# One pinned split instead of two in the expert stage of a hybrid mLSTM / RWKV-7 / MoE layer

## The chip, the cores and the metric

The kernel runs on one core of a Trainium2 chip. The metric is the device time of one execution in microseconds (us), with the median over several runs. Beside the times there is one profiled execution, whose trace gives each instruction's start and duration on TensorE (matrix products), VectorE, ScalarE, GpSimd and SyncE (which issues most transfers).

## The reference, cut to what matters

The layer is a backbone layer over 2048 latent tokens of 1024 channels with 256 context tokens: a modulated layer norm, one input projection, an mLSTM group and an RWKV-7 group, an output projection, and then a mixture of experts. The change touches only the last of these. There are 32 experts; each token goes to two of them, with weights `w`:

```python
    def expert_block(args):
        idx, w, e = args
        xb = tok_pad[idx]
        hb = jax.nn.silu(xb @ ex_gate[e]) * (xb @ ex_up[e])
        return (hb @ ex_down[e]) * w[:, None]
...
    y = lax.map(expert_block, (tok_buf.reshape(n_blk, MOE_BLOCK), w_buf.reshape(n_blk, MOE_BLOCK), blk_exp))
    out = jnp.zeros((n + 1, d), y.dtype).at[tok_buf].add(y.reshape(buf, d))
```

`ex_gate[e]` and `ex_up[e]` are 1024 x 512, `ex_down[e]` is 512 x 1024, all in float32. The result of each expert's block is added to its tokens' rows, and a layer norm follows.

## The kernel before, in words

**Precision.** A float32 product is made from three products of rounded halves. Each operand A is split into a high part H (a copy on ScalarE that rounds) and a low part L = A - H (a subtraction on VectorE); the product is H·H + H·L + L·H, three matmuls on TensorE, added up in one PSUM tile.

**Weights.** An expert has six raw tiles of 1 MB (gate 2, up 2, down 2), which SyncE loads from HBM into a pool of seven (`ER`), each when an earlier tile of the pool has been used up. Each raw tile gives two pieces of 128 x 1024 (`split`, lines 1525 to 1533: the copy is line 1531, the subtraction line 1532), so an expert has twelve: 0 to 3 for gate, 4 to 7 for up, 8 to 11 for down. H and L parts lie in pools of thirteen buffers each (`EH`), so piece i of an expert takes the buffer of piece i-1 of the expert before.

**An expert's round.** `moe` loops over the 32 experts in Python, fully unrolled. For a block of 128 gathered tokens, `gate_up` makes the gate product (8 steps over the channels), the Silu on ScalarE into `act`, and the up product in two column halves. When the first up half is complete, `mult(0)` on VectorE multiplies it into `act` (line 1622); two transposes of that half on TensorE, the copy `aH` on ScalarE and the subtraction `aL` on VectorE (lines 1540, 1548, 1553) make the operand for the first two steps of the down product. `mult(1)` does the same for the second half. `tail` makes the down product in four steps, each with one down piece, with the transposes of the next expert's tokens (`fill`) after the first step; the result is scaled and added to the tokens' rows in HBM by GpSimd (`add`).

**More than 128 tokens.** Where an expert has more tokens, further blocks run with the same pieces inside a runtime branch (`tc.If(nx > 0)`, line 1737) that stands between `gate_up` and the tail of the last block. Every engine passes this branch. In the data used, twelve of the 32 experts take it, and some of these have more than one further block.

**Order.** Every engine works through its own queue in order. A planner (the framework's scheduler) puts the instructions of the straight code in that order by its own estimates of when each is ready; among instructions that are ready, what is traced earlier stands to go first. The program forces it in places: `behind()` and `tc.issue_after(ins)` put what is traced inside them behind `ins` on the engine of `ins` alone, and on no other engine.

**Where the pieces are split.** At the end of a round, pieces 0 to 7 of the next expert are traced (`AHEAD` is 8): 0 and 1 in no forced place, 2 to 7 behind the last split of `act`. At the start of the next round the pieces up to number 9 follow in no forced place (line 1706). The rest, pieces 10 and 11, come from `more(2, m)` in `gate_up` (line 1609): their VectorE subtractions are pinned behind `m`, which is `mult(0)`; their ScalarE copies are not.

Of the kernel before, what the change touches and what calls it, by code (L numbers as in the profile page):

```python
# [53 lines left out]
class Kern:  # L54
# [1442 lines left out]
    def moe(self):  # L1497
        tc, nc, I, s = self.tc, self.nc, self.I, self.scratch
        with ExitStack() as es:
# [25 lines left out]
            def split(R, i):  # L1525

                w = R[i // 2]
                hk = w.shape[1] // 2
                w = w[:, hk * (i % 2):hk * (i % 2) + hk, :]
                H, L = hp.tile(list(w.shape), FR, name="eH"), hp.tile(list(w.shape), FR, name="eL")  # L1530
                self.cp = nc.scalar.copy(H, w)  # L1531
                nc.vector.tensor_tensor(L, w, H, op=OP.subtract)  # L1532
                return H, L

            def split_T(A, src, g, step, own=False, after=None, later=False):

                ps = (pu if own else pt).tile([128, 4, 128], F, name="epx" if own else "ept")
                for k in range(step):
                    kk = step * g + k
                    self.pe = nc.tensor.transpose(ps[:, k, :], src[:, 128 * kk:128 * kk + 128], self.ident)  # L1540
                    if after:
                        tc.add_manual_dep(self.pe.ins, after.ins.name,
                                          mybir.DependencyInfo(mybir.DependencyClass.NoSync, mybir.DependencyReason.DATA),
                                          reason="the expert's own products go first")
                ks = slice(step * g, step * g + step)

                def split(order=None):
                    self.lastc = nc.scalar.copy(A[0][:, ks], ps[:, :step])  # L1548
                    if order:
                        tc.add_manual_dep(self.lastc.ins, order.ins.name,  # L1550
                                          mybir.DependencyInfo(mybir.DependencyClass.NoSync, mybir.DependencyReason.DATA),
                                          reason="the block's own work goes first")
                    self.last = nc.vector.tensor_tensor(A[1][:, ks], ps[:, :step], A[0][:, ks], op=OP.subtract)  # L1553

                if later:
                    return split
                split()

            def parts(pool, n, nm):
                return tuple(pool.tile([128, n, 128], FR, name=nm + x, bufs=1) for x in "HL")  # L1560

            def mm(o, A, W, k, kw, c, first, last):
                H, L = W
                for i, (a, b) in enumerate(((A[0], H), (A[0], L), (A[1], H))):
                    self.pe = nc.tensor.matmul(o, a[:, k, :], b[:, kw, c], start=first and i == 0, stop=last and i == 2)  # L1565

            def behind():

                return tc.issue_after(self.pe.ins) if self.pe else ExitStack()
# [6 lines left out]
            def load_ids(dst, src):  # L1576
                ld = nc.gpsimd.dma_start(dst, src)
                for sc in self.scat:
                    behind_dma(ld, sc, "entries of the token table")

            def gather(x, ids):
                return nc.gpsimd.indirect_dma_start(out=x, out_offset=None, in_=self.H2,
                                                    in_offset=bass.IndirectOffsetOnAxis(ap=ids, axis=0))

            def gate_up(X, W, R=None):

                def more(n, behind):
                    if R:  # L1590
                        with tc.issue_after(behind.ins):
                            for _ in range(n):
                                W.append(split(R, len(W)))

                g = pu.tile([128, DE], F, name="epg")
                for k in range(8):
                    mm(g, X, W[k // 2], k, k % 2, slice(0, DE), k == 0, k == 7)
                nc.scalar.activation(act, g, AF.Silu)

                def up(k, h):  # L1600
                    mm(us[h][:, 0:256], X, W[4 + k // 2], k, k % 2, slice(256 * h, 256 * h + 256), k == 0, k == 7)

                for k in range(3):
                    for h in range(2):
                        up(k, h)
                for k in range(3, 8):
                    up(k, 0)
                m = mult(0)
                more(2, m)
                with behind():  # L1610
                    for k in range(3, 6):
                        up(k, 1)
                with behind():
                    split_T(Aa, act, 0, 2)
                with behind():
                    for k in range(6, 8):
                        up(k, 1)
                mult(1)

            def mult(h):  # L1620
                c = act[:, 256 * h:256 * h + 256]
                return nc.vector.tensor_tensor(c, c, us[h][:, 0:256], op=OP.mult)
# [36 lines left out]
            Rs = {0: load_raw(0)}  # L1659
            W = [split(Rs[0], i) for i in range(AHEAD)]  # L1660
# [36 lines left out]
            for e in range(NE):  # L1697
                nx, x1 = coming

                with behind():  # L1700
                    tc.mark_branch_hint_location("e%d" % e, hint=nx, engines=[PE])
                cur = ids[:, 0, e]
                act = bp.tile([128, DE], F, name="act")
                Aa = parts(bp, 4, "a")
                us = [pu.tile([128, 512], F, name="epu%d" % h) for h in range(2)]
                W += [split(Rs[e], i) for i in range(len(W), 10)]
                if left:
                    add(*left)
                with behind() if e == 0 else ExitStack():
                    gate_up(X, W, Rs[e])  # L1710
                last = self.pe

                def extra(i):


                    if not isinstance(i, int) or i > 1:
                        new = ap.tile([128, 2], I32, name="more")
                        load_ids(new, self.TB[bass.ds((i + (16 * e + 1)) * 128, 128), :])
                        gather(x1, new[:, 0:1])
                    else:  # L1720
                        new = ids[:, 1 + i, e]
                    old = ap.tile([128, 2], I32, name="old")
                    nc.vector.tensor_copy(old, cur)
                    nc.vector.tensor_copy(cur, new)
                    self.pe = None
                    Z = parts(xp, 8, "z")

                    def mid():
                        with tc.If(nx > 1):
                            gather(x1, ids[:, 2, e, 0:1])  # L1730

                    add(tail(W, lambda g: split_T(Z, x1, g, 4, later=g == 0), mid if isinstance(i, int) and i == 0 else None), old)
                    gate_up(Z, W)

                if e + 1 < NE:
                    coming = begin(e + 1, order)
                with tc.If(nx > 0, label="e%d" % e):  # L1737
                    tc.mark_branch_hint_location("f%d" % e, hint=nx - 1, engines=[PE])
                    extra(0)
                    with tc.If(nx > 1, label="f%d" % e):  # L1740
                        extra(1)
                        with tc.If(nx > 2):
                            with tc.For_i(2, nx, 1) as i:
                                extra(i)

                def fill(g):
                    nonlocal x
                    if e + 1 < NE:
                        late = split_T(X, x, g, 4, True, last, g == 0)
                    else:  # L1750
                        late = None
                    if g == 1 and e + 2 < NE:
                        x = fetch(ids[:, 0, e + 2, 0:1])
                    return late

                self.pe = None
                X = parts(xp, 8, "x")
                left = tail(W, fill), cur
                order = self.last
                if e + 2 < NE:  # L1760
                    Rs[e + 2] = load_raw(e + 2)
                if e + 1 < NE:
                    W = [split(Rs[e + 1], i) for i in range(2)]
                    with tc.issue_after(self.evac[0]), tc.issue_after(self.evac[1]):
                        W += [split(Rs[e + 1], i) for i in range(2, AHEAD)]
# [84 lines left out]
```

## Time and profile before

| | |
|---|---|
| median of 3 runs | 3421.06 us (3416.99 to 3427.79) |
| profiled execution: its time / its span | 3418.58 us / 3417.0 us |
| TensorE (matmul) busy | 2866.9 us, 84% |
| VectorE busy | 2339.6 us, 68% |
| ScalarE busy | 1364.0 us, 40% |
| GpSimd busy | 879.0 us, 26% |
| expert stage in the trace | about 2305 to 3351 us |
| splits in it, line 1531 / line 1532 | 384 x 1052 ns / 384 x 1221 ns |

Busy shares are averages over stages with different limits. The expert stage is read by itself, in windows of one expert's round. In a timeline row the numbers are the start and the length in us, and the bracket gives the idle time of the engine before the instruction and what ended it. "xN" in a row means N instructions in a row, merged. Where a suffix q stands behind an engine's name, it is that engine's sequencer, which takes branches and sends semaphore events.

### The profile page before, as it was taken

To read this page: it belongs to the slowest core of one execution; us is meant where nothing else is said; L and a number is where in the kernel's file an instruction comes from. 1 tells how busy PE (TensorE), PEld (TensorE's weight loads), DVE (VectorE), ACT (ScalarE), POOL (GpSimd) and SP (SyncE) were. 2 spreads that over 40 slices of the span, in tenths; PEclk is the share of its full clock that TensorE was granted. 3 is DMA by queue.
4 is the path that set the end of the run, shared out by engine and by line. 5 is a ranking of instruction groups with operands and counts; after the bars stand their busy time and mean duration, and the time that the engine had idled before them with its cause. 6 is when DMAs were issued, how large, how long until landed. Compare 5 with 4: busy or idle time off the path is not lost. (4 is left out here: it accounts for less than half of the span.)

```text
span 3417.0 us, 61401 instructions
## 1 busy us (share of the span) xinstructions
PE 2866.9 (84%) x24042; PEld 2405.9 (70%) x24042; DVE 2339.6 (68%) x3822; ACT 1364.0 (40%) x2187; POOL 879.0 (26%) x862
## 2 busy tenths in 40 slices
PE   6899999999979964777777588859899989989992
PEld 3677788898757754666666567647778877878781
DVE  4488888766787875667656288875877736476447
ACT  4432322335545322334344233344655525355233
POOL 5400000013455660112112365431222212122210
PEclk9899999999979875778788789979999999999996
DMA  5333332235468534666664554448988848597535
GB/s 187 117 114 108 101 116 82 88 101 189 164 219 242 167 109 115 171 159 170 155 168 128 159 174 137 141 147 286 334 295 284 304 125 276 159 335 234 177 112 209
DMA packets 471689, 602.59 MB, mean 176 GB/s; under 512 B 127222, under 2 KB 312338, under 8 KB 471314
## 3 DMA queue, kind: packets, MB, share of 16 engines
q1 hardware_dynamic: 413617, 441.15, 41.2%
q0 software_dynamic: 36736, 129.33, 13.0%
q10 hardware_dynamic: 20960, 27.20, 2.5%
q8 instruction: 224, 3.67, 0.5%
q14 instruction: 152, 1.24, 0.1%
HBM read 453.24 MB, written 144.33 MB: 175 GB/s over the span
## 5 line engine op out<-in xcount | busy, mean ns | idle before, releaser
L1532 DVE TENSOR_TENSOR eL<-eraw,eH 128x1024 fp32r<-128x1024 f32 x384 | 449.6, 1221 | 28.6 <-ACT eH L1531 24.6
L329 DVE SCALAR_TENSOR_TENSOR cacc<-P,cw,cacc 128x1008 f32<-128x1008 f32 (+3 forms) x320 | 398.7, 1247 | 56.5 <-ACT cacc L304 45.6
L1531 ACT CAST eH<-eraw 128x1024 fp32r<-128x1024 f32 x384 | 370.9, 1052 | 48.3 <-PEq L1737 35.1
L263 PE MATMUL in_ps<-hH,w_H 128*128 128x512 f32 (+1 forms) x664 | 252.3, 382 | 1.7 <-ACT pl_ev L355 1.7
L263 PE MATMUL in_ps<-hL,w_H 128*128 128x512 f32 (+1 forms) x664 | 249.6, 377 | 0.0
L263 PE MATMUL in_ps<-hH,w_L 128*128 128x512 f32 (+1 forms) x664 | 248.0, 374 | 0.0
L1565 PE MATMUL epo<-eH,aH 128*128 128x512 f32 x408 | 172.2, 422 | 64.8 <-DVEq L1737 32.2
L1651 POOL DMA_INDIRECT ACC<-yo,ids x32 | 131.0, 4093 | 250.5 <-DVE yo L1650 226.1
L1565 PE MATMUL epo<-eH,aL 128*128 128x512 f32 x408 | 159.7, 404 | 11.7 <-DVE aL L1553 11.7
L1565 PE MATMUL epo<-eL,aH 128*128 128x512 f32 x408 | 163.2, 400 | 0.0
L931 PE MATMUL rpg<-KR,BK 64*128 64x128 f32 (+1 forms) x1152 | 122.4, 350 | 46.7 <-ACT BT L941 17.5
L237 POOL DMA_DIRECT2D w_raw<-in_w_in x28 | 21.2, 757 | 506.2 <-DVE w_L L251 371.8
L263 PEld LDWEIGHTS in_ps<-hH,w_H 128*128 128x128 f32 x664 | 126.2, 191 | 34.6 <-issue 11.5
L931 PEld LDWEIGHTS rpg<-KR,BK 64*128 64x128 f32 x1152 | 104.9, 248 | 63.2 <-issue 23.8
L973 DVE TENSOR_TENSOR sT<-sM,sY 128x31 f32<-128x31 f32 (+15 forms) x279 | 95.3, 342 | 78.8 <-DMA sM<-BL 70.8
L298 ACT COPY P<-in_ps 128x512 f32<-128x512 f32 (+1 forms) x92 | 51.3, 557 | 235.8 <-PE in_ps L263 235.8
L1565 PE MATMUL epu<-eH,xL 128*128 128x256 f32 x512 | 143.4, 283 | 0.0
L1565 PE MATMUL epu<-eL,xH 128*128 128x256 f32 x512 | 143.2, 283 | 0.0
L263 PEld LDWEIGHTS in_ps<-hL,w_H 128*128 128x128 f32 x664 | 126.2, 190 | 22.7 <-issue 2.1
L1565 PE MATMUL epu<-eH,xH 128*128 128x256 f32 x512 | 142.2, 288 | 0.0
L263 PEld LDWEIGHTS in_ps<-hH,w_L 128*128 128x128 f32 x664 | 126.1, 190 | 22.3 <-issue 0.8
L1565 PEld LDWEIGHTS epo<-eH,aH 128*128 128x128 f32 x408 | 78.9, 193 | 83.1 <-ACT xH L1548 30.7
(471 smaller groups left out, 8151.1 us busy)
## 6 DMA issues: line engine op xcount, KB each, us to landing
eraw<-in_ex_gate SPq DMA_DIRECT2D x64, 1024.0 KB
eraw<-in_ex_up SPq DMA_DIRECT2D x64, 1024.0 KB
eraw<-in_ex_down SPq DMA_DIRECT2D x64, 1024.0 KB
pk<-PK SPq DMA_DIRECT2D x144, 320.0 KB
PK<-pk POOLq DMA_DIRECT2D x36, 768.0 KB, 3.9
ada_w<-in_w_ada SPq DMA_DIRECT2D x32, 512.0 KB
v<-MV SPq DMA_DIRECT2D x50, 264.0 KB
kc<-KTd SPq DMA_DIRECT2D x50, 256.0 KB
```

Source lines behind the costliest of these rows:

```text
L237: self.wld = nc.gpsimd.dma_start(w[:, 4:8, o:o + cn], src[:, 4:8])
L263: nc.tensor.matmul(o, a[:, k, :], b, start=i == 0, stop=i == 3 * KT - 1)
L298: nc.scalar.copy(P[:, t0:t0 + n], ps)
L329: nc.vector.scalar_tensor_tensor(o, img[:, r0 + sy:r1 + sy, c0 + sx:c1 + sx], wt(dy, dx), o, op0=OP.mult, op1=OP.add)
L931: nc.tensor.matmul(pG[e][:, q, b.cols], b.BK[HD[e], c, q, :], b.KR[HD[e], c, q, b.cols], start=True, stop=True, tile_position=(64 * e, 0))
L973: nc.vector.tensor_tensor(tt, M[:, 0:j, j:j + 1].to_broadcast([128, j, w]), Y[:, j:j + 1, j:32].to_broadcast([128, j, w]), op=OP.mult)
L1531: self.cp = nc.scalar.copy(H, w)
L1532: nc.vector.tensor_tensor(L, w, H, op=OP.subtract)
L1565: self.pe = nc.tensor.matmul(o, a[:, k, :], b[:, kw, c], start=first and i == 0, stop=last and i == 2)
L1651: nc.gpsimd.indirect_dma_start(out=self.ACC, out_offset=bass.IndirectOffsetOnAxis(ap=cur[:, 0:1], axis=0), in_=y, in_offset=None, compute_ ...
```

## The change

One number goes from 2 to 1 and one from 10 to 11. In `gate_up`, one piece (11) and not two has its subtraction pinned behind `mult(0)`. At the start of a round, three pieces (8, 9 and 10) and not two are traced in no forced place, ahead of `add` and `gate_up`. Nothing is computed differently, and the number of instructions stays the same.

```diff
@@ gate_up
                 for k in range(3, 8):
                     up(k, 0)
                 m = mult(0)
-                more(2, m)
+                more(1, m)
                 with behind():
                     for k in range(3, 6):
                         up(k, 1)
@@ the loop over the experts
                 us = [pu.tile([128, 512], F, name="epu%d" % h) for h in range(2)]
-                W += [split(Rs[e], i) for i in range(len(W), 10)]
+                W += [split(Rs[e], i) for i in range(len(W), 11)]
                 if left:
                     add(*left)
```

The function that `gate_up` calls for the pinned pieces, unchanged:

```python
def more(n, behind):
    if R:
        with tc.issue_after(behind.ins):
            for _ in range(n):
                W.append(split(R, len(W)))
```

## Rows read from the trace of the kernel before

**Rows 1.** Windows of one round: length, busy per engine, PEclk, DMA share, GB/s.
```profile
2425.70:2446.30 20.60, 18.25 (x110) 15.95 (x110) 17.86 (x21) 13.68 (x17) 5.54 (x3) 1.00 1.04 355
...
2671.50:2692.20 20.70, 18.35 (x111) 16.02 (x110) 17.89 (x22) 13.68 (x17) 7.61 (x4) 1.00 1.04 374
```

**Rows 2.** Waits of TensorE, expert stage: who waited for whom, us, times, longest.
```profile
PE epo L1565 <- DVEq L1737: 32.2, 14, 2.4
PE epo L1565 <- PEq L1737: 14.8, 3, 5.1
...
PE epo L1565 <- DVE aL L1553: 11.7, 12, 1.0
PE epo L1565 <- ACT eH L1531: 7.0, 3, 2.4
```

**Rows 3.** Timeline of the last expert, VectorE, ScalarE and TensorE.
```profile
3342.20 2.35 DVE L1532 TENSOR_TENSOR eL<-eraw,eH 128x1024 fp32r<-128x1024 f32 x2
...
3343.09 0.37 ACT L1548 CAST aH<-ept 128x256 fp32r<-128x256 f32 x1 [3.77 <-PE ept L1540]
...
3344.47 0.42 DVE L1553 TENSOR_TENSOR aL<-ept,aH 128x256 fp32r<-128x256 f32 x1
...
3345.42 0.47 PE L1565 MATMUL epo<-eH,aH 128*128 128x512 f32 x1 [1.66 <-DVEq L1737]
```

**Rows 4.** Timeline of an expert with a further block, TensorE's wait.
```profile
2574.97 0.50 PE L1565 MATMUL epo<-eH,aL 128*128 128x512 f32 x1 [0.97 <-DVE aL L1553]
```

**Rows 5.** Timeline of a round without a further block, from mult(0) on.
```profile
2466.97 0.42 DVE L1622 TENSOR_TENSOR act<-act,epu 128x256 f32<-128x256 f32 x1 [1.05 <-PE epu L1565]
...
2467.31 3.49 DVE L1532 TENSOR_TENSOR eL<-eraw,eH 128x1024 fp32r<-128x1024 f32 x3
...
2467.78 0.38 PE L1540 MATMUL ept<-ident,act 128*128 128x128 f32 x2
...
2468.20 0.37 ACT L1548 CAST aH<-ept 128x256 fp32r<-128x256 f32 x1 [2.82 <-PE ept L1540]
...
2470.72 0.42 DVE L1553 TENSOR_TENSOR aL<-ept,aH 128x256 fp32r<-128x256 f32 x1
2471.05 0.41 DVE L1622 TENSOR_TENSOR act<-act,epu 128x256 f32<-128x256 f32 x1
...
2471.66 0.47 PE L1565 MATMUL epo<-eH,aH 128*128 128x512 f32 x1 [2.35 <-DVEq L1737]
...
2475.65 0.40 PE L1565 MATMUL epg<-eH,xL 128*128 128x512 f32 x1
...
2476.09 2.36 DVE L1532 TENSOR_TENSOR eL<-eraw,eH 128x1024 fp32r<-128x1024 f32 x2 [0.16 <-ACT eH L1531]
```

**Rows 6.** Line 1737 (the branch) in that round: duration ns, first and last start.
```profile
L1737 PEldq EVENT_SEMAPHORE  x1: 51/51/51, 2469.4 to 2469.4; - x1
...
L1737 DVEq EVENT_SEMAPHORE  x1: 21/21/21, 2471.5 to 2471.5; - x1
```

**Rows 7.** Timeline of the copies and of VectorE ahead of mult(0); last expert's copies.
```profile
2617.59 10.54 ACT L1531 CAST eH<-eraw 128x1024 fp32r<-128x1024 f32 x11
2628.03 0.59 ACT L1598 ACTIVATE act<-epg 128x512 f32<-128x512 f32 x1
...
2625.69 3.49 DVE L1532 TENSOR_TENSOR eL<-eraw,eH 128x1024 fp32r<-128x1024 f32 x3
2630.22 0.42 DVE L1622 TENSOR_TENSOR act<-act,epu 128x256 f32<-128x256 f32 x1 [1.04 <-PE epu L1565]
...
3329.23 9.60 ACT L1531 CAST eH<-eraw 128x1024 fp32r<-128x1024 f32 x10
```

**Rows 8.** Windows of 2 us after a 2.35 us wait, columns as in rows 1.
```profile
2494.00:2496.00 2.00, 2.00 (x9) 1.67 (x9) 0.08 (x1) 0.33 (x1) 0.09 (x1) 0.50 0.99 308
2496.00:2498.00 2.00, 2.00 (x8) 1.57 (x7) 1.55 (x4) 2.00 (x4) 0.91 (x1) 0.69 1.05 410
```

**Rows 9.** Timeline of SyncE: issue of the next gate's two tiles.
```profile
2612.32 3.50 SPq L1518 DMA_DIRECT2D eraw<-in_ex_gate  x2
```

## The prediction, made before the change was run

> **What bounds the kernel now.** The profiled execution takes 3418.58 us, 1.58 us of it outside its span of 3417.0; the median of the three runs shown is 3421.06, so 2.48 is added at the end. The diff touches the expert stage alone, about 2305 to 3351 us. I read the busy time by window first, to see what an expert's round is made of. A round of an expert without a further block (20 of the 32) takes 20.6 us, of which TensorE is busy 18.25 and VectorE 17.86, at the full 2.4 GHz clock, while the DMA share stands above 1 [rows 1]. So three things are nearly full and none is quite full; what decides is the wait between two of them.
>
> The view of waits says which. TensorE waits 32.2 us in 14 pieces for VectorE's queue at line 1737, the branch around the further block, 7.0 us in three pieces put down to a copy on ScalarE, and 11.7 us in twelve pieces for `aL` [rows 2]. The single waits show what the totals hide: every one of the first two kinds is 2.35 us, in 16 experts, but for the last expert's 1.66 [rows 3]; each of the twelve experts with a further block waits 0.97 or 0.98 [rows 4]; and three experts wait for TensorE's own branch, 14.8 us in all [rows 2], where nothing on VectorE matters.
>
> The timeline of one round shows the 2.35 [rows 5]. `mult(0)` starts on VectorE at 2466.97. Behind it stand three subtractions of a split, 3.49 us together, then `aL`, then `mult(1)`, and only when that is over does VectorE pass the branch: its semaphore event is at 2471.5, TensorE's own at 2469.4 [rows 6]. TensorE starts the down products at 2471.66. ScalarE's `aH` had ended at 2468.57, so `aL`, and `mult(1)` behind it, stood about 2.1 us behind splits that the block doesn't need yet. The three late "ScalarE" waits start TensorE 0.61 us after `mult(1)` as the others do, so I count them as the same wait.
>
> **Which three splits these are.** ScalarE makes eleven copies without a gap and then the Silu [rows 7]; in the last expert, which has no successor, it makes ten, and only two subtractions stand behind `mult(0)` [rows 3, 7]. So the eleventh copy, and the third subtraction, is piece 0 of the next expert, and the other two are pieces 10 and 11, which `more(2, m)` pins there. Pieces 8 and 9, free, were put ahead of `mult(0)`.
>
> **The change, part by part.** *The pin.* `issue_after` holds only VectorE's half of a split, so ScalarE's copies were free before and need not move. One subtraction loses its pin. I expect the planner to treat piece 10 as it treated piece 9: it is traced ahead of `gate_up`, its copy is done before the Silu on which `mult(0)` depends, and its buffer (thirteen per half) is that of piece 9 of the expert before, last read in that expert's tail.
>
> *What leaves the path.* Three subtractions take 3.49 us, two take 2.35 [rows 3, 5], so the burst shortens by 1.14.
>
> *What it costs ahead of `mult(0)`.* VectorE is idle there for 1.04 us, waiting for the up products [rows 7]. That idle time is the cover: 1.14 goes into it, and `mult(0)` starts 0.10 later. The transposes that read it start 0.39 us after its end [rows 5], so TensorE does not feel the 0.10; the burst does. Were the cover gone, `mult(0)` would be late by 1.14 and the gain would be nil, since the burst is shorter by as much. Queued behind piece 10 on VectorE are only `mult(0)` and the burst.
>
> *Rounds without a further block.* 1.14 - 0.10 = 1.04 us off each 2.35; sixteen of them give 16.6. The last expert keeps one subtraction of two, but `aL` can't start before `aH` ends (3343.46; it started 1.0 later, behind two subtractions) [rows 3]: 0.95. The last expert is also the test of the step, with the planner's own order: with two subtractions its TensorE waits 1.66 and not 2.35, the 1.14 less but for some 0.45 in which it transposes nothing for a successor.
>
> *Rounds with a further block.* TensorE stands 0.97 for `aL` [rows 4]; `aL` comes 1.04 earlier, so the wait goes: 12 x 0.97 = 11.6. What follows on VectorE there (`mult(1)`, the `zL` halves) moves up with it.
>
> *The three branch waits.* Nothing: they end later than VectorE does.
>
> Sum: 16.6 + 0.95 + 11.6 = 29.2 us.
>
> *Clock.* After five of the sixteen 2.35 us waits TensorE is granted 1.2 GHz for a time. In the one shown two windows of 2 us have 0.50 and 0.69 of full speed, so 1.0 + 0.6 = 1.6 us are lost [rows 8]; five make 8. After the waits of 0.97, of 1.66 and the other ones under 1.8 us it stays at 2.4 GHz throughout. The new waits are 1.3 us, between these, nearer to those without a fall. Bounds 0 and 8; I take 5.
>
> *Transfers.* SyncE's loads are issued when VectorE frees a raw tile, so they come in the same order, each 1 us closer to the next. The round that moves 355 GB/s in 20.6 us (7.3 MB) must then move it in 19.6, 373 GB/s. One round already runs at 374 [rows 1]. What covers a shortfall is the lead of the loads: the tightest, the next gate's first tile, is issued at 2612.32 [rows 9] and copied as the eleventh of the row that begins at 2617.59 and lasts 10.54 [rows 7], so at about 2627: 14.7 us. It and the pair ahead of it, three tiles of 1.05 MB, take about 9 us at 355 GB/s from the earlier issue, so it lands near 2618 and some 9 us are spare. If the DMA can't go faster at all, each round falls 1 us behind; the longest run of rounds without a further block is seven, and a further block lets the loads catch up. Bounds: nothing, and all of the 16.6; I take 2, because the spare time is larger than seven rounds ask for.
>
> The Trainium skill speaks against the change here: "DMA: Bandwidth & Descriptors" (the warning on its three ceilings) has the HBM side, about 358 GB/s per core, bind such loads. By that a round of 7.3 MB needs 20.4 us, and the rounds would give only 0.2 us each once the lead is eaten. The round at 374 does not agree with it as a hard limit.
>
> So 29.2 + 5 - 2 = 32.2: 3418.58 - 32.2 = 3386.4 for the profiled execution, and 2.48 more, **3389 us**, for a median.
>
> **The rivals.** *The planner leaves the order as it is* (10%). If its estimate has `mult(0)` ready before VectorE is through with piece 9, and it takes what is ready by another measure than trace order, piece 10 stays behind `mult(0)` with or without a pin: the same three subtractions, 3421. For it: the next expert's piece 0 was as free as piece 9 and stands behind `mult(0)`. Against it: that piece is traced later than `mult(0)`, piece 10 earlier.
>
> *The loads become the bound* (10%). If the spare 9 us are not there, the rounds stay at 20.6 us, ScalarE waits for the gate's tile in front of the Silu, and only the further blocks and the last expert gain: 12.5 us, 3408.5, right at the edge of what can be told. For it: the DMA share of 1.04 in these rounds [rows 1]. Against it: the gapless row of copies [rows 7], and 374 GB/s.
>
> *Slower, by the gate's products* (8%). TensorE fills the tail with gate products of the next expert; at 2475.65 they run on while VectorE begins pieces 2 and 3 at 2476.09 [rows 5]. Pieces 0 and 1 give ten more products of about 0.23 us, until 2477.9; piece 2 is ready at 2477.3. If the changed plan drew piece 2's products straight to 2475.65, TensorE would wait 1.65 us in every expert: 32 x 1.65 = 53, less the 29 gained, 3421 + 24 = 3445. It decides from 0.9 us per expert on. Against it: the pin that is lost lies 9 us away from these products, and their order needs no change.
>
> **How the numbers follow.** The forecast has 72%, the three rivals 10, 10 and 8. A median of this kernel can be told from no change by about 0.3%, 10.3 us. The forecast lies beyond that, and I give half of the second rival to faster and half to same: faster 0.77, same 0.15, slower 0.08. The likeliest case's own range is 3382 (all 8 of the clock, no loss to the loads) to 3396 (nothing from the clock, 4 lost to the loads). The range takes in the rivals up to no change and the spread of its runs, 3424, and goes to 3378 for a gain that I sized too small; it leaves out the slower rival and a little below.
>
> **What would show it.** Right: two subtractions in one row behind `mult(0)` (2.35 us) and four instead of three ahead of it; TensorE's waits at line 1737 near 1.3 us sixteen times; no wait for `aL` in the twelve; rounds of 19.6 us; fewer windows below full clock; idle before `mult(0)` near zero. Wrong: still three subtractions behind `mult(0)`; waits of ScalarE's copies for the gate's transfer, with gaps in its row of eleven; a new wait of gate products for `eL`; a rise of the idle time before the transposes of `act`, which would say that the 1.04 of cover was less than I took it for.

## The result, and the profile after

The changed kernel takes 3385.86 us (median of 4 runs, 3376.78 to 3389.73) against 3422.27 for the kernel before (4 runs, 3416.99 to 3427.79): a ratio of 0.9894, interval 0.9869 to 0.9919, or 36.4 us less. 3389 was forecast. The profiled execution took 3376.78 us with a span of 3375.1; 9 us of its distance to the one before lie ahead of the expert stage, where nothing was changed, and are the spread of single executions. So I compare the stage by itself. From the first down product of the first expert to that of the last it took 3345.42 - 2322.48 = 1022.9 us before and 3303.34 - 2313.39 = 990.0 after, 32.9 less. The 3.5 us that the medians differ by beyond this are not accounted for; executions of the changed kernel alone lie up to 13 us apart.

The timeline of a round without a further block, from the last splits ahead of `mult(0)` on (it answers to [rows 5, 7]; SyncE, GpSimd, weight loads and the up products are left out):

```profile
2447.70 4.62 DVE L1532 TENSOR_TENSOR eL<-eraw,eH 128x1024 fp32r<-128x1024 f32 x4
2452.26 0.42 DVE L1622 TENSOR_TENSOR act<-act,epu 128x256 f32<-128x256 f32 x1
2452.60 2.35 DVE L1532 TENSOR_TENSOR eL<-eraw,eH 128x1024 fp32r<-128x1024 f32 x2
2453.07 0.38 PE L1540 MATMUL ept<-ident,act 128*128 128x128 f32 x2
2453.48 0.37 ACT L1548 CAST aH<-ept 128x256 fp32r<-128x256 f32 x1 [2.85 <-PE ept L1540]
...
2454.87 0.41 DVE L1553 TENSOR_TENSOR aL<-ept,aH 128x256 fp32r<-128x256 f32 x1
2455.20 0.41 DVE L1622 TENSOR_TENSOR act<-act,epu 128x256 f32<-128x256 f32 x1
...
2455.81 0.47 PE L1565 MATMUL epo<-eH,aH 128*128 128x512 f32 x1 [1.21 <-ACT eH L1531]
```

Four subtractions in a row stand ahead of `mult(0)` and two, 2.35 us, behind it. `mult(0)` follows them with no idle time. TensorE starts the down products 0.61 us after the start of `mult(1)`, as before [rows 5], and has waited 1.21 us instead of 2.35. The view names ScalarE's `eH` as the releaser. That copy, of the next expert's piece 1, ran from 2454.73 to 2455.77, so by this round alone it could be. A kernel further below settles it: with piece 1 moved elsewhere, fifteen such waits are 1.21 to 1.27 us long still, and the view puts them down to VectorE at line 1737.

Three windows of a round (against [rows 1]; busy time of TensorE, weight loads, VectorE, ScalarE, GpSimd, then clock, DMA share, GB/s). The first starts at an expert whose wait was ended by TensorE's own branch:

```profile
2435.31:2455.81 20.50, 18.56 (x108) 15.82 (x109) 17.81 (x22) 14.59 (x19) 6.71 (x2) 1.00 1.04 366
2455.81:2475.38 19.57, 18.32 (x109) 15.98 (x109) 17.82 (x22) 13.72 (x18) 6.70 (x2) 1.00 1.04 366
2475.38:2494.91 19.53, 18.32 (x109) 15.97 (x109) 17.75 (x22) 13.65 (x18) 8.73 (x3) 1.00 1.04 373
```

A regular round takes 19.53 to 19.57 us, 1.1 less than before; the first of the three, with a wait of 0.73 for `xL` in it, takes 20.50. And the view of TensorE's waits in the stage (against [rows 2]):

```profile
PE epo L1565 <- PEq L1737: 20.9, 7, 5.0
...
PE epo L1565 <- ACT eH L1531: 14.7, 12, 1.2
...
PE epx L1540 <- DVE xL L1553: 7.7, 16, 0.7
...
PE epo L1565 <- DVEq L1737: 0.7, 1, 0.7
```

The wait for `aL` is gone. Of the sixteen waits of 2.35 us twelve are now 1.21 to 1.25. The other four stand in the first row, which had three entries before and has seven: experts 5, 12, 19 and 26 now wait 1.48 to 1.75 us for TensorE's own branch, and each of them waits 0.73 more for `xL` a little later. The last row is the last expert, 0.69 instead of 1.66 [rows 3].

ScalarE's row of copies has no gap in this round, so no load came late. In the whole stage one copy waits for a load, the eleventh of the row that ends the longest run of rounds without a further block (last line):

```profile
2439.60 10.54 ACT L1531 CAST eH<-eraw 128x1024 fp32r<-128x1024 f32 x11
2450.03 0.60 ACT L1598 ACTIVATE act<-epg 128x512 f32<-128x512 f32 x1
...
2508.61 1.05 ACT L1531 CAST eH<-eraw 128x1024 fp32r<-128x1024 f32 x1 [0.73 <-DMA eraw<-in_ex_gate]
```

And the clock does not fall after the new waits. This is one of the four longest, 1.73 us up to 2435.31, and the four microseconds behind it, where [rows 8] had 0.50 and 0.69:

```profile
2433.60:2435.30 1.70, 0.00 (x0) 0.02 (x1) 0.99 (x3) 0.16 (x1) 0.00 (x0) 1.00 1.03 408
2435.30:2437.30 2.00, 1.99 (x8) 1.32 (x8) 1.08 (x1) 1.37 (x2) 0.00 (x0) 1.00 1.06 308
2437.30:2439.30 2.00, 1.27 (x9) 1.10 (x9) 0.74 (x2) 0.45 (x1) 0.21 (x1) 1.00 1.06 272
```

### The profile page after: what moved, and what is told of

Same layout as the page of the kernel before. It is cut to its first block, busy times and chain, and to the rows that moved or that the text cites. A ratio compares the mean times of both kernels' runs of the same rounds, so it can differ in the third digit from the quotient of the medians.

```text
span 3375.1 us, 61432 instructions
## 1 busy us (share of the span) xinstructions
PE 2854.0 (85%) x24042; PEld 2395.2 (71%) x24042; DVE 2337.1 (69%) x3822; ACT 1364.7 (40%) x2187; POOL 926.2 (27%) x862
## 3 DMA queue, kind: packets, MB, share of 16 engines
q14 instruction: 153, 1.25, 0.1%
## 5 line engine op out<-in xcount | busy, mean ns | idle before, releaser
L1651 POOL DMA_INDIRECT ACC<-yo,ids x32 | 175.2, 5476 | 240.7 <-DVE yo L1650 240.7
L1582 POOL DMA_INDIRECT xg<-H,ids x48 | 59.6, 1242 | 246.4 <-PE ept L1540 192.4
```

The lines of the kernel that those rows point to most:

```text
L1651: nc.gpsimd.indirect_dma_start(out=self.ACC, out_offset=bass.IndirectOffsetOnAxis(ap=cur[:, 0:1], axis=0), in_=y, in_offset=None, compute_ ...
```

## The experiments

My theory: VectorE's burst behind `mult(0)` sets the wait of each round, and VectorE's idle time ahead of `mult(0)` is what can take a split out of it. Rivals: the length of the burst alone decides, wherever the rest stands; or the gain comes from somewhere else in the stage. Each kernel is set against the kernel before, run beside it on the same chip; each diff is against the changed kernel, unless another is named.

**The change in two halves.** One kernel has it only in the twelve experts with a further block, one only in the other twenty.

```diff
-                more(1, m)
+                more(12 - len(W), m)
...
-                W += [split(Rs[e], i) for i in range(len(W), 11)]
+                W += [split(Rs[e], i) for i in range(len(W), 11 if e in FURTHER else 10)]
```

(`FURTHER` stands for the set 1, 9, 10, 15, 16, 18, 20, 21, 25, 28, 29, 30; the other half has `not in`.)

> The change is made only in the twelve experts that take the further block; the other twenty keep two pinned pieces and ten in no forced place. Theory (each kind of round gains by itself, by the burst behind mult(0)): the twelve waits of 0.97 us for aL go, the sixteen of 2.35 us stay, and with them the falls of the clock: about 12 us faster than before, 3410. Rival (the gain is the planner's new order of gate and down products on TensorE inside the further blocks, which the change brought along): most of the 36 us come here, 3390. Rival (what is gained in one kind of round is lost again at the next wait): no change.

Measured: 3409.92 us (median), ratio 0.9974, interval 0.9962 to 0.9987, 11.9 us less than the 3421.8 before.

> The change is made only in the twenty experts that do not take the further block. Theory: the sixteen waits of 2.35 us shrink to 1.2, except that the four rounds whose branch on TensorE comes late gain little; the clock stays up behind the shorter waits; the twelve waits of 0.97 us stay. About 21 us faster than before (11 from the waits, 1 from the last expert, up to 8 from the clock), 3401, and with the kernel of the other half of the experts it adds up to the whole gain. Rival (order of TensorE's products in the further blocks): nearly nothing, 3420.

Measured: 3397.38 us, ratio 0.9943, interval 0.9921 to 0.9964, 24.4 less. The two gains add up to 36.3, the whole is 36.4. The intervals of the two gains are about 4 and 7 us to either side, so the closeness is luck; but the gain has the two independent sources that the prediction named, and no third one larger than these intervals. TensorE's waits in the second half show the first source used and the second not:

```profile
PE epo L1565 <- ACT eH L1531: 14.6, 12, 1.2
PE epo L1565 <- DVE aL L1553: 11.6, 12, 1.0
```

**Other numbers of splits behind `mult(0)`.** The kernel before has three in a row there and the changed one two, the next expert's piece 0 among them. First, four:

```diff
-                more(1, m)
+                more(3, m)
...
-                W += [split(Rs[e], i) for i in range(len(W), 11)]
+                W += [split(Rs[e], i) for i in range(len(W), 9)]
```

> The opposite dose: three pieces pinned behind mult(0) and nine in no forced place, so four subtractions instead of three stand behind mult(0). Theory: each of the sixteen waits grows from 2.35 to 3.5 us, the twelve for aL from 0.97 to 2.1, the last expert's by 1.1: 33 us slower than before, and up to 10 us more because the clock falls after more of the longer waits: 3455 to 3465. Rival (only the wait at mult(0) counts, and it has slack): no change from before, 3422.

Measured: 3482.47 us, ratio 1.0175, interval 1.0155 to 1.0196. The waits came as expected, and the time did not:

```profile
PE epo L1565 <- DVEq L1737: 62.0, 18, 3.5
PE epo L1565 <- DVE aL L1553: 25.3, 12, 2.1
```

Seventeen waits of 3.48 (the eighteenth is the last expert's 2.79) and twelve of 2.1. What I had set too small was the clock, here in a window of one such wait and the four microseconds behind it:

```profile
2433.26:2436.74 3.48, 0.00 (x1) 0.03 (x1) 3.33 (x6) 1.53 (x2) 0.00 (x0) 1.00 1.02 303
2436.74:2438.74 2.00, 2.00 (x7) 1.61 (x8) 1.77 (x2) 0.00 (x0) 0.00 (x0) 0.74 0.97 305
2438.74:2440.74 2.00, 2.00 (x10) 1.70 (x8) 0.00 (x0) 0.18 (x1) 0.00 (x0) 0.50 1.14 354
```

The grant falls to the lower level, 1.2 GHz, after 14 of the 17 waits of 3.48 and after 11 of the 12 of 2.1. So a split more behind `mult(0)` costs its own 1.14 per round, and the clock on top.

Then none: no piece of the expert's own is pinned, and the next expert's piece 0 stays free.

```diff
-                more(1, m)
+                more(0, m)
...
-                W += [split(Rs[e], i) for i in range(len(W), 11)]
+                W += [split(Rs[e], i) for i in range(len(W), 12)]
```

> No piece pinned and twelve in no forced place; the planner then also draws the next expert's piece 0 ahead of mult(0), so no subtraction at all stands behind it. Theory (what was won is bounded by VectorE's idle time ahead of mult(0), which the change has used up): mult(0) comes 2.3 us later than after the change, the burst ends only 1.0 earlier, so a round takes 20.9 us and the experts with a further block stand 1.9 us before the transposes of act; 40 us slower than after the change, 3425. Rival (the burst alone counts): another 1.1 us off each round, 25 to 30 us faster than after the change, 3358.

Measured: 3448.01 us, ratio 1.0079, interval 1.006 to 1.0099: slower than before, where 3425 was expected. The planner put six splits ahead of `mult(0)`, the next expert's piece 0 among them, and none behind (the profiled execution, of 3471.76 us, is the longest of its five):

```profile
2484.00 6.89 DVE L1532 TENSOR_TENSOR eL<-eraw,eH 128x1024 fp32r<-128x1024 f32 x6
2490.80 0.41 DVE L1622 TENSOR_TENSOR act<-act,epu 128x256 f32<-128x256 f32 x1
2492.15 0.42 DVE L1553 TENSOR_TENSOR aL<-ept,aH 128x256 fp32r<-128x256 f32 x1 [0.94 <-ACT aH L1548]
```

TensorE's wait has moved from the branch to the transposes of `act`, which wait for `mult(0)`. A wait of 0.7 us for `xL` has come in, 27 times, which I had not counted. It is a part of the 23 us by which I was off, 14.9 in all where the change has 7.7 already; the rest I did not take apart:

```profile
PE ept L1540 <- DVE act L1622: 54.2, 31, 1.8
...
PE epx L1540 <- DVE xL L1553: 14.9, 27, 0.7
...
PE epo L1565 <- DVEq L1737: 4.6, 13, 0.7
```

The wait at line 1737 has all but gone, and the kernel is slower than before: the length of the burst is not what decides.

And one: the next expert's piece 0 alone, pinned.

```diff
-                more(1, m)
+                if R: self.m0 = m
...
-                W += [split(Rs[e], i) for i in range(len(W), 11)]
+                W += [split(Rs[e], i) for i in range(len(W), 12)]
...
-                    W = [split(Rs[e + 1], i) for i in range(2)]
+                    with tc.issue_after(self.m0.ins): W = [split(Rs[e + 1], 0)]
+                    W += [split(Rs[e + 1], i) for i in range(1, 2)]
```

> One step further than the change: all of pieces 8 to 11 are traced in no forced place, and the next expert's piece 0 alone is pinned behind mult(0), so that five subtractions stand ahead of mult(0) and one behind it. Theory 1 (VectorE's idle time ahead of mult(0) was the cover, and the change has used it up: 1.04 us before, none after): the fifth subtraction makes mult(0) late by its whole 1.14 us, so the burst of one gains nothing, and the late transposes of act put a wait of their own into each round; as in the run without any pin, a wait of some 0.7 us for xL is added. Rounds of about 20.3 us, against 19.55 for the change; some 24 us slower than the change, about 3410. Theory 2 (what sets the wait is the length of the burst behind mult(0), wherever the rest stands): TensorE's waits at line 1737 go from 1.2 to about 0.1 us and the kernel takes about 3365.

Measured: 3410.9 us, ratio 0.9969, interval 0.9952 to 0.9986. Theory 1 said 3410, theory 2 3365. With five splits ahead of `mult(0)` and one behind, TensorE waits at three places of a round:

```profile
PE ept L1540 <- DVE act L1622: 18.8, 31, 0.7
PE epx L1540 <- DVE xL L1553: 16.3, 28, 0.7
...
PE epo L1565 <- DVEq L1737: 5.0, 13, 0.7
```

So the order of the doses, by splits in a row behind `mult(0)`: none 3448, one 3411, two (the change) 3386, three (before) 3422, four 3482. By this number alone there is nothing more to gain.

**Moving a split to another place.** In the changed kernel the one idle time of VectorE above 0.2 us in a round is ahead of the second half of `xL`:

```profile
2439.47 0.69 DVE L1553 TENSOR_TENSOR xL<-epx,xH 128x512 fp32r<-128x512 f32 x1 [1.43 <-ACT xH L1548]
```

One kernel has piece 1 of the next expert pinned behind the first half of `xL` and `xH`, on both engines, and nothing else:

```diff
-                                late(self.pe)
+                                late(self.pe); self.x0 = self.last.ins, self.lastc.ins
...
-                    W = [split(Rs[e + 1], i) for i in range(2)]
+                    W = [split(Rs[e + 1], 0)]
+                    with tc.issue_after(self.x0[0]), tc.issue_after(self.x0[1]): W += [split(Rs[e + 1], 1)]
```

> The change as it is, with one split moved: piece 1 of the next expert is pinned, on VectorE and on ScalarE, behind the first half of the transposed tokens (xL, xH), into the 1.4 us in which VectorE stands idle between the two halves of xL. The burst behind mult(0) stays at two. Theory 1 (in the four rounds in which TensorE comes late through its own branch, the second wait of 0.73 us for xL arises because piece 1 of the next expert stands ahead of xL): these four waits go, 0.73 x 4 = 2.9 us, and a regular round gains at most 0.1 us: 3 to 6 us faster than the change, about 3381. Theory 2 (xL is late there for the transposes alone): the four waits stay and the time is that of the change, 3386.

Measured: 3365.57 us, ratio 0.9842, interval 0.9819 to 0.9866: the fastest kernel here, 20 us below the change. That is several times what I expected, and only part of it for the reason given. Its waits in the stage:

```profile
PE epo L1565 <- DVEq L1737: 19.2, 16, 1.3
...
PE epo L1565 <- ACT xH L1548: 7.6, 9, 1.7
...
PE epo L1565 <- DVE xL L1553: 5.9, 3, 2.0
PE epo L1565 <- PEq L1737: 2.1, 1, 2.1
```

The waits of the transposes for `xL` are gone, all 7.7 us of them and not the 2.9 of four experts alone. The three entries for `xL` and the one for the branch are the four late experts, whose waits in front of the down product have grown from 6.6 to 8.0 us, so 6.3 of the 7.7 are gained. What I had not expected is that the three waits of 4.7 to 4.95 us for TensorE's branch, in experts 3, 17 and 24, are 1.24 to 1.27 now, some 10.6 us less, and that the falls of the clock behind them are gone with them (two have come in behind the four late experts). A regular round is 19.48 to 19.50 us, hardly shorter than the change's. VectorE's idle time ahead of the second half of `xL` did not fill, it is 1.41 us still: piece 1 now stands between the first half and that idle time, where it stood ahead of the first half.

The two edits together, one split behind `mult(0)` and piece 1 behind the first `xL`:

> Both of the two edits: one subtraction behind mult(0) instead of two, and piece 1 of the next expert moved into VectorE's idle time between the halves of xL, so that there is again one subtraction fewer ahead of mult(0). Theory 1 (the change's rule goes on as long as mult(0) is not late): mult(0) starts on time, the wait at line 1737 falls from 1.2 to about 0.1 us, rounds take about 18.6 us, and the kernel takes about 3370. Rival (the loads become the bound): a round moves 7.3 MB, which in 18.6 us is 393 GB/s, above the 374 seen so far; then ScalarE's row of eleven copies shows gaps in front of the next gate's tile and the rounds stay at 19.3 us or more: 3382 or above. Second rival (the cover is used up all the same, since the rounds get shorter by as much as VectorE was relieved): mult(0) is late, and the time is that of the change, 3386.

Measured: 3373.95 us, ratio 0.9859, interval 0.9836 to 0.9883. That is no gain over the kernel with piece 1 moved alone (their intervals overlap), and the second rival holds in its mechanism, though not in its time: `mult(0)` is late, TensorE's transposes wait some 0.64 us for it in 31 experts. The timeline of VectorE and the window of that round:

```profile
2396.76 5.75 DVE L1532 TENSOR_TENSOR eL<-eraw,eH 128x1024 fp32r<-128x1024 f32 x5
2402.43 0.41 DVE L1622 TENSOR_TENSOR act<-act,epu 128x256 f32<-128x256 f32 x1
2402.76 1.22 DVE L1532 TENSOR_TENSOR eL<-eraw,eH 128x1024 fp32r<-128x1024 f32 x1
```

```profile
2385.37:2404.84 19.47, 18.48 (x108) 16.06 (x109) 17.88 (x21) 13.69 (x18) 7.83 (x2) 1.00 1.04 357
```

Five splits stand ahead of `mult(0)` without a gap, one behind, and the round is 19.47 us, as with two behind.

A last kernel of this kind has one split behind `mult(0)`, no new pin for piece 1, and piece 2 of the next expert in a free place beside pieces 0 and 1 (this diff is against the kernel above with piece 0 alone pinned):

```diff
-                    W += [split(Rs[e + 1], i) for i in range(1, 2)]
+                    W += [split(Rs[e + 1], i) for i in range(1, 3)]
...
-                        W += [split(Rs[e + 1], i) for i in range(2, AHEAD)]
+                        W += [split(Rs[e + 1], i) for i in range(3, AHEAD)]
```

> One subtraction behind mult(0), five ahead of it, and piece 2 of the next expert given a free place beside pieces 0 and 1, for VectorE's idle time between the halves of xL, instead of the pin behind the last split of act. Theory 1 (idle time counts only where it lies ahead of mult(0)): piece 2 leaves the end of the round for its middle, which makes room for one subtraction ahead of the next mult(0), so that mult(0) is late by little; rounds of about 19.0 us, about 3378. Theory 2 (TensorE reads the pieces so soon that filling the slot delays xL): waits of about 0.7 us for xL in each round, rounds of about 20 us, about 3400.

Measured: 3390.89 us, ratio 0.9922, interval 0.9893 to 0.9952, between the two theories. A round (from 2469.33 to 2488.88, the restarts after `xL`) takes 19.55 us, with a wait of 0.73 for `xL` and some 0.3 at the branch: again the same round with its wait at another place.

**Why some branches take long.** The view of line 1737 gives the branch of TensorE itself, duration in ns. In a regular expert, then in expert 5 and in expert 3 of the changed kernel:

```profile
L1737 PEldq COMPARE_BRANCH  x1: 355/355/355, 2452.9 to 2452.9; - x1
...
L1737 PEldq COMPARE_BRANCH  x1: 3132/3132/3132, 2431.9 to 2431.9; - x1
...
L1737 PEldq COMPARE_BRANCH  x1: 6112/6112/6112, 2387.3 to 2387.3; - x1
```

The long branches come every seven experts. To see whether that is a matter of where the branch lies in TensorE's instructions, I put transposes of 32 x 32 that nobody reads ahead of the stage, where TensorE waits some 20 us for the first tokens; all that follows lies further along.

```diff
+            pads = [pt.tile([128, 4, 128], F, name="ept") for _ in range(2)]
+            for i in range(18):
+                nc.tensor.transpose(pads[i % 2][0:32, 0, 0:32], self.ident[0:32, 0:32], self.ident[0:32, 0:32])
```

> The changed kernel with 18 transposes of 32 x 32 added on TensorE ahead of the expert stage, where it stands idle for some 20 us waiting for the first tokens; their result is read by nobody. Everything that TensorE executes in the expert stage lies 18 transposes further along its instruction stream and is otherwise the same but for a few exchanged places. Theory 1 (TensorE's branch at line 1737 is slow, 6.1 us in experts 3, 17 and 24 and 3 us in 5, 12, 19 and 26, because of where it lies in the stream, whose pattern repeats every seven experts): the slow branches change, to other experts or to other lengths, and the time with them, between 3370 (no branch of 6 us) and 3400. Theory 2 (what those experts do at that moment, their loads or their tokens, makes it slow): the same branches of 6.1 and 3 us in the same experts, and 3386.

Measured: 3378.51 us, ratio 0.987, interval 0.9845 to 0.9895.

> The same with 64 such transposes. Theory 1: the slow branches are others again than with 18 and than with none, still the same ones modulo seven; between 3370 and 3400. Theory 2: 6.1 us in experts 3, 17 and 24 and 3 us in 5, 12, 19 and 26, and 3386.

Measured: 3378.47 us, ratio 0.9867, interval 0.9843 to 0.9891.

> The kernel in which piece 1 of the next expert is moved into VectorE's idle time between the halves of xL, with the same 64 transposes ahead of the stage. It had no branch of 6 us and took 3365.6, 20 us less than the change, where 3 to 6 less were expected. Theory 1 (some 15 us of that gain came from branches of TensorE that were no longer slow, by their place in the instruction stream): the slow branches change again, and the time goes to between 3365 and 3385. Theory 2 (the moved split itself made the branches fast): no branch of 6 us, 3366.

Measured: 3366.91 us, ratio 0.9838, interval 0.9806 to 0.987.

The branches of over 0.6 us in each kernel, read expert by expert in the same view (the twelve experts with a further block fall through the branch in 70 to 82 ns and don't count):

| kernel | about 6 us | 2.3 to 3.5 us | 0.6 to 2 us |
|---|---|---|---|
| before | 3, 17, 24 | 5, 12, 19, 26 | 14 |
| changed | 3, 17, 24 | 5, 12, 19, 26 | 0, 7, 14 |
| changed, 18 transposes | 8, 22 | 3, 17, 24 | 5, 12, 19, 31 |
| changed, 64 transposes | 4, 11 | 6, 13, 27 | 8 |
| piece 1 moved | none | 5, 12, 19, 26 | 0, 7, 14 |
| piece 1 moved, 64 transposes | none | 6, 13, 22, 27 | 8 |

With 18 transposes expert 3, for one, goes from 6.1 to 3.4 us, and expert 8 now has 6.2:

```profile
L1740 PEldq COMPARE_BRANCH  x1: 6212/6212/6212, 2494.3 to 2494.3; - x1
...
L1740 PEldq COMPARE_BRANCH  x1: 3402/3402/3402, 2394.3 to 2394.3; - x1
```

So theory 1 holds for which experts have the long branches: but for a few exchanged places, nothing but the place of the instructions was changed, and the pattern, with its distance of seven, moved along. But it is not all. The moved piece 1 takes away the branches of 6 us in both places that were tried, as its theory 2 had it (and in the kernel with one split behind `mult(0)` besides, where experts 3, 17 and 24 have 350 to 398 ns), and leaves the ones of 3 us; and the time did not go up with the 64 transposes. The transfers show a difference between the two kinds. Within the branch of 3.1 us that begins at 2431.9 an instruction transfer of 16 KB begins in the half microsecond from 2432.25 on, within the one of 6.1 us that begins at 2387.3 only in that from 2390.5 on (columns: packets, MB, share):

```profile
q8 instruction: 1, 0.02, 13.2%
```

```profile
q8 instruction: 1, 0.02, 14.1%
```

The other branches in the two columns of the table are like them: in all of 2.3 to 3.5 us the transfer begins 0.3 to 1.1 us into the branch, in all of about 6 us 3.4 to 4.2. The long kind is thus the short one, with its transfer some 3 us later. What makes it late, and why moving one split on VectorE and ScalarE ends that, no run here shows.

## Why the prediction was right, point by point

*The planner's order.* Four subtractions ahead of `mult(0)`, two behind it, idle time gone, as forecast; the rival by which the planner leaves the order fell.

*Rounds without a further block, 16.6 us forecast.* Twelve waits went from 2.35 to about 1.22, 13.5 us in all, a little more each than the 1.04 forecast, since `mult(0)` is not 0.10 later but some 0.05 (15.98 and 16.02 us behind the restart in two rounds, 15.92 and 15.97 before). The other four gained nothing: 2.35 before; 1.73, 1.75, 1.62 and 1.48 now, each with 0.73 for `xL` behind it. This is the step that failed in its size. I had read the three waits that were put down to ScalarE [rows 2] as "the same wait", because TensorE started 0.61 us after `mult(1)` there too. The view of line 1737 in the kernel before shows what it was that stood just below it in expert 5:

```profile
L1737 PEldq COMPARE_BRANCH  x1: 2815/2815/2815, 2446.9 to 2446.9; - x1
...
L1737 PEldq EVENT_SEMAPHORE  x1: 51/51/51, 2449.8 to 2449.8; - x1
L1737 DVEq EVENT_SEMAPHORE  x1: 21/21/21, 2450.8 to 2450.8; - x1
```

TensorE's event comes 1.0 us ahead of VectorE's, and not 2.1 as in [rows 6]. Taking 1.1 us from VectorE brings TensorE's own branch to the front. The 0.73 for `xL` comes from ScalarE: its copy of the next expert's piece 1 waits for TensorE's event (idle 2.30 us there, 0.87 in a regular round), and the copy `xH` stands behind it. In expert 5 of the changed kernel:

```profile
2435.14 1.05 ACT L1531 CAST eH<-eraw 128x1024 fp32r<-128x1024 f32 x1 [2.30 <-PEq L1737]
2436.09 0.58 ACT L1548 CAST xH<-epx 128x512 fp32r<-128x512 f32 x1
```

*Last expert, 0.95 forecast:* 0.97. *Further blocks, 11.6 forecast:* the 11.7 us of waits for `aL` are gone, and the half with this alone gained 11.9.

*Clock, 5 forecast between 0 and 8:* no fall is left after any of these waits, all five are gone, at 1.6 each (an estimate from the one in [rows 8]) the full 8. How many of the sixteen waits have a fall differs between traces: the half with further blocks alone has the same sixteen, and three falls.

*Loads, 2 forecast between 0 and 16.6:* nothing. A round of 19.53 us moved 373 GB/s without a gap in the copies, so the rival by which the loads become the bound fell. It fell narrowly: the 9 us that I took to be spare were used up over the seven rounds of the longest run, at whose end the one copy waits 0.73 us for its tile. That round was no longer for it: from its restart to the next branch it has 16.62 us, the two rounds ahead of it 16.63 and 16.59. With piece 1 moved the same copy waits 1.54. The rule that I had set against the change is that of the Trainium skill, "DMA: Bandwidth & Descriptors" (Where 436 GB/s comes from, the warning on its three ceilings): about 358 GB/s per core is what binds. With rounds at 366 to 373 GB/s it does not hold here as a hard limit. "HBM Reference" of the Trainium skill (Specifications) has a core that streams alone measure well above that share, about 425 GB/s. This kernel runs on one core, and its rounds do lie above the share; no run here shows the 425.

*The sum.* 13.5 + 0.97 + 11.7 + 8 = 34.2, against 32.2 forecast. Of the stage's interval that I measured, the first expert's wait (1.14) lies ahead, and the two waits for further tokens grew from 11.7 to 12.8; so 34.2 - 1.1 - 1.1 = 32.0 where 32.9 were measured. Two errors of size, the late branches (3.1 too much) and the clock (3 too little), cancelled, which was luck; the 2 set aside for the loads are what is left.

*The slower rival* fell: TensorE's gate products start in the tail as they did, and no wait for `eL` came in.

*What bounds the round now.* The experiments point to more than the prediction had asked: it seems to be VectorE. A round of 19.57 us has 17.82 of its work, and its idle times in it are 1.43 ahead of `xL` and twice 0.2 or less for `eH`. Before, a round had 1.04 more, ahead of `mult(0)` [rows 7]; that is what the change took, and all it could take. The three kernels with a round of 19.47 to 19.55 and the wait at three different places agree with that. It is not shown: no kernel here gives VectorE less to do, and with one load 0.73 us late at this pace, the loads stand close behind as a bound.

## What to carry to other kernels

Where an engine makes another wait behind a burst, moving work out of the burst gains only what idle time there is ahead of it: sum up that engine's busy and idle time over one round, and stop when the idle time is used up, for the next step only moves the wait. For each wait that is to shrink, look in every occurrence at what ended second last, by how much, and not at one example: a near tie in four of sixteen took a quarter of that term here. A branch can be such a second-last, and its length can depend on where it lies.

## What the runs showed that I had not expected

TensorE's branch at line 1737, over the code of the further blocks, takes 0.35 us in most experts and 3 or 6 us in some, seven experts apart; 18 small transposes ahead of the stage moved the long branches to other experts. The stage was 982.5 us then against 990.0; the medians differ by as much, but their intervals overlap.

The granted clock does not follow the length of a wait alone. After waits of up to 1.75 us it did not fall in any of the changed kernel's rounds; after 2.1 in front of the third down product it fell 11 times of 12, after 2.35 in front of the first one 5 times of 16 (the kernel before), after 3.48 there 14 times of 17. In front of the transposes of `act`, 1.8 were followed by a fall 11 times of 30 (the kernel with no piece behind `mult(0)`).

The version with piece 1 moved is the best one found, 3365.57 us, 0.9842 of the kernel before, with and without the added transposes (3366.91). Of its 20 us below the change, 6.3 are waits for `xL`, with what the four late experts lost taken off, and some 10.6 the shorter branches; the rest may be the clock behind them, which I did not take apart. Why the branches became shorter stays open.
